# A transformer block on one core: the transposes of the softmax weights of three query heads put side by side, and their value products in the unit behind

## The chip, the cores and the metric

The kernel runs on one core of one Trainium2 chip. The metric is the device time of one execution in microseconds (us). The engines are named as the profile names them: PE (matrix products, with PEld for loading its weights), DVE (vector), ACT (scalar), POOL, and SP, which issues most DMAs. Each engine works through its own queue in order, and waits in that queue where an instruction needs the result or the freed buffer of another.

## The reference

One layer of an encoder block over 256 tokens of width 2048, in float32. Cut to what the change touches:

```python
h = rmsnorm(x); q, k, v, u = split(h @ w_in)        # 12 query heads, 4 key heads, 128 wide
scores = q @ k.T * HEAD_DIM**-0.5 - slope * |t - s|  # only |t - s| <= 128
m = max(max(scores), sink); p = exp(scores - m)
p = p / (sum(p) + exp(sink - m))
a = rmsnorm(p @ v)                                   # three query heads share a key head
f = rmsnorm(fourier_mix(u))
x = x + concat(a, f) @ w_out
x = x + conv_ffn(rmsnorm(x)); return rmsnorm(x)
```

Nothing in the mathematics is changed.

## The kernel before, in words

Every product is made of float32 halves: a weight tile of 128 x 2048 arrives by DMA, ACT rounds it to a high half and DVE subtracts to get the low half (`split`, lines 185 and 186), and PE multiplies high by high, high by low and low by high. The front of the program, up to about 215 us, is a list of numbered *units*. A unit is one such weight tile and the PE work on it. Units 4 to 7 make the values, units 8 to 23 project one key or query head each, in the order k0 q0 q1 q2 k1 q3 q4 q5 k2 q6 q7 q8 k3 q9 q10 q11 (so q3 is unit 13, q4 unit 14, q5 unit 15, k2 unit 16), and units 24 to 39 are the output projection. Behind them comes the feed-forward part, which the change does not touch.

The order is written by hand. Around the products of unit i three lists are run: `before` (PE work placed ahead of them), `beside` (the ACT and DVE work of the steps), then the split of the weights of unit i+2, then `behind`. A query head h whose projection is unit s passes through these steps:

- `qk_out` and `qk_parts` beside unit s+1: the sum `add` and the two halves of `qT`, on ACT and DVE.
- `scores` before unit s+2: six products into a bank `ps_s`; `scores_out` (DVE) beside it, and `exps` (ACT) behind it, leave the exponentials in a tile `sc`.
- `weigh` beside unit s+3: DVE divides `sc` by its sum.
- `turn` before unit s+4: four PE transposes of `sc` into a bank `ps_t` (line 712); `turn_out` beside it: ACT copies the bank to the high half `pt0`, DVE subtracts for the low half `pt1` (lines 724 and 725).
- `values` before unit s+5: six products into a bank `ps_o` (line 734); `values_out` beside it: a square on ACT that POOL adds up (lines 491 and 496), and the two halves of `cat` on ACT and DVE (lines 234 and 235), which the output projection reads.

PSUM has eight banks, in two pools of four: `mm` and `dn`. The projections take `mm`; the scores, the transposes and small sums such as `ps_totf` (the sum of squares of the Fourier part, before unit 15) take `dn`. A tile asked of a pool that has no free buffer takes the one that is freed first, and its first instruction waits for the last reader of the old tile.

Of the kernel before, what the change touches and what calls it, by code (L numbers as in the profile page):

```python
# [9 lines left out]
F32R = mybir.dt.float32r  # L10
# [3 lines left out]
P = 128  # L14
# [6 lines left out]
GQA = 3  # L21
# [30 lines left out]
N_OUT = N_QK + len(QK_ORDER)  # L52
# [44 lines left out]
def block_kernel(  # L97
# [24 lines left out]
    mm = ctx.enter_context(tc.tile_pool(name="mm", bufs=4, space=bass.MemoryType.PSUM))  # L122
    dn = ctx.enter_context(tc.tile_pool(name="dn", bufs=4, space=bass.MemoryType.PSUM))

    def f32(ap):
        return ap.bitcast(F32)
# [182 lines left out]
    ph = pa.enter_context(tc.tile_pool(name="pa", bufs=1))  # L309
# [103 lines left out]
    before, beside, behind = {}, {}, {}  # L413

    def at(when, i, f, *a):
        when.setdefault(i, []).append((f, a))
# [215 lines left out]
    def qk_out(kind, h, ps):  # L632
        tmp = ph.tile([P, S], F32, tag="tmp", name=f"tmp_{kind}{h}", bufs=2)
        nc.scalar.activation(tmp, ps[:, S : 2 * S], AF.Copy)
        add = ph.tile([P, S], F32, tag="add", name=f"add_{kind}{h}", bufs=2)
        nc.vector.tensor_tensor(add, ps[:, 0:S], tmp, ALU.add)
        if kind == "k":
            nc.vector.tensor_tensor(add, add, r1b, ALU.mult)
        st["add", kind, h] = add
# [77 lines left out]

    def turn_out(h):
        ps = st.pop(("t", h))
        pt = [  # L720
            ph.tile([P, 512], F32R, tag=f"pt{q}", name=f"pt{q}{h}", bufs=2)
            for q in range(2)
        ]
        nc.scalar.activation(pt[0], ps, AF.Copy)
        nc.vector.tensor_tensor(pt[1], ps, f32(pt[0]), ALU.subtract)
        st["p", h] = pt
# [20 lines left out]
    slot_of = {kh: N_QK + n for n, kh in enumerate(QK_ORDER)}  # L747
    for i in range(N_QK, N_OUT + 8):
        heads = {i - s: h for (kind, h), s in slot_of.items() if kind == "q"}
        new = [kh for kh, s in slot_of.items() if i - s == 1]  # L750
        if i - 9 in range(NG):
            at(before, i, fourier_channels, i - 9)
        if 5 in heads:
            at(before, i, values, heads[5], mm if i < N_OUT else dn)
        if 4 in heads:
            at(before, i, turn, heads[4])
        if i == 15:
            at(before, i, total, sq_f, "f")
        if 2 in heads:
            at(before, i, scores, heads[2])  # L760

        for kind, h in new:
            if kind == "q":
                at(beside, i, lambda k=kind, h=h: qk_out(k, h, st.pop(("ps", k, h))))
        if 4 in heads:
            at(beside, i, turn_out, heads[4])
        if 3 in heads:
            at(beside, i, weigh, heads[3])
        for kind, h in new:
            if kind == "k":  # L770
                at(beside, i, lambda k=kind, h=h: qk_out(k, h, st.pop(("ps", k, h))))
            at(beside, i, qk_parts, kind, h)
        if 2 in heads:
            at(beside, i, scores_out, heads[2])
            at(behind, i, exps, heads[2])
        if 5 in heads:
            at(beside, i, values_out, heads[5])

    fourier_channels_steps()
    for n, (kind, h) in enumerate(QK_ORDER):  # L780
# [57 lines left out]
    for n, (c, kq) in enumerate(OUT_ORDER):  # L838
        i = N_OUT + n
# [391 lines left out]
    i = up_index[n]  # L1231
# [156 lines left out]
```

## Time and profile before

| | |
|---|---|
| median of 3 runs | 906.06 us (905.99 to 906.23) |
| the profiled execution | 906.14 us, of which the span of the trace is 904.4 us |
| PE busy | 895.6 us, 99% |
| DVE, ACT, POOL busy | 745.1 us (82%), 547.2 us (61%), 51.7 us (6%) |
| HBM read | 211.93 MB, 237 GB/s over the span |

The stretch that the change touches, units 13 to 28, lies between about 80 and 185 us. In the rows of the timeline the columns are the start, the duration, engine, line, operation, the tiles (out<-in, with head numbers left out), the shape and a count; a bracket at the end names idle time ahead of the instruction and what ended it. Durations of PE overlap, since its products are pipelined: what one costs is read from the distance between starts.

### The profile page before, as it was taken

What the parts mean: (1) busy time and instruction counts of PE and PEld (TensorE: products, weight loads), DVE (VectorE), ACT (ScalarE), POOL (GpSimd) and SP (SyncE); (2) the same over time, 40 slices, a digit from 0 to 9 for tenths busy, and PEclk for the clock granted to TensorE, in tenths of its full rate; (3) what the DMA queues carried; (4) which work ended last, traced back from release to release, by engine and by line L of the source; (5) the groups of instructions that cost most, each with busy time, mean ns of one, the idle gap of its engine ahead of it and who ended that gap; (6) DMA issues with size and microseconds to landing.
All of it is one profiled execution on the core that took longest, in us unless ns stands there. A gap on an engine that the chain in (4) does not pass through costs nothing.

```text
span 904.4 us, 12754 instructions
## 1 busy us (share of the span) xinstructions
PE 895.6 (99%) x5073; PEld 811.1 (90%) x5073; DVE 745.1 (82%) x892; ACT 547.2 (61%) x663; POOL 51.7 (6%) x65
## 2 busy tenths in 40 slices
PE   9999999999999999999999999999999999999996
PEld 8899999888899999999999999999999999999885
DVE  7579888666668877889887998878988789998996
ACT  7767677555454656556565565566655566656544
POOL 0001111000000000000000000000000000000004
PEclk9999999999999999999999999999999999999999
DMA  9864544456568678677898779887787988779652
GB/s 365 332 234 145 187 152 175 146 180 226 192 231 283 231 242 251 188 257 230 275 266 271 245 258 287 258 276 237 275 250 245 312 263 262 242 240 286 217 196 94
DMA packets 32908, 214.86 MB, mean 238 GB/s; under 512 B 3632, under 2 KB 4016, under 8 KB 8528
## 3 DMA queue, kind: packets, MB, share of 16 engines
q1 hardware_dynamic: 28448, 183.89, 54.5%
q0 software_dynamic: 4112, 29.49, 17.1%
q8 instruction: 40, 0.66, 0.3%
q10 hardware_dynamic: 288, 0.66, 0.2%
q14 instruction: 20, 0.16, 0.0%
HBM read 211.93 MB, written 2.10 MB: 237 GB/s over the span
## 4 chain that ended last, share of the span: by engine, by line
PE 95%; DVE 2%; POOL 1%; issue 1%; ACT 0%; POOLq 0%; ACTq 0%; DVEq 0%
PE ps_val L394 17%; PE ps_gate L394 17%; PE ps_gate L396 8%; PE ps_val L396 8%; PE ps_q L394 5%; PE ps_P L1105 3%; PE ps_P L1107 3%; PE ps_P L1106 3%; PE ps_N L1105 2%; PE ps_N L1107 2%; PE ps_N L1106 2%; PE ps_u L286 2%; PE ps_q L396 2%; PE ps_a L377 2%; PE ps_a L379 2%; PE ps_a L378 2%
## 5 line engine op out<-in xcount | busy, mean ns | idle before, releaser
L186 DVE TENSOR_TENSOR parts<-raw,parts 128x2048 fp32r<-128x2048 f32 (+1 forms) x129 | 293.2, 2273 | 49.4 <-ACT parts L185 48.9
L185 ACT ACTIVATE parts<-raw 128x2048 fp32r<-128x2048 f32 (+1 forms) x129 | 245.4, 1902 | 46.7 <-PE ps_a L379 12.4
L394 PE MATMUL ps_val<-hU,parts 128*128 128x512 f32 x688 | 227.7, 382 | 0.0
L394 PE MATMUL ps_gate<-hU,parts 128*128 128x512 f32 x688 | 227.3, 382 | 0.0
L396 PE MATMUL ps_val<-hU,parts 128*128 128x256 f32 x688 | 187.5, 273 | 0.0
L396 PE MATMUL ps_gate<-hU,parts 128*128 128x256 f32 x688 | 186.9, 273 | 0.0
L394 PEld LDWEIGHTS ps_val<-hU,parts 128*128 128x128 f32 x688 | 130.0, 189 | 18.1
L394 PEld LDWEIGHTS ps_gate<-hU,parts 128*128 128x128 f32 x688 | 130.0, 189 | 18.1
L396 PEld LDWEIGHTS ps_val<-hU,parts 128*128 128x128 f32 x688 | 132.0, 192 | 0.8
L396 PEld LDWEIGHTS ps_gate<-hU,parts 128*128 128x128 f32 x688 | 131.8, 192 | 0.9
L883 ACT ACTIVATE ft_g<-ps_gate 128x256 f32<-128x256 f32 x43 | 16.5, 384 | 112.7 <-PE ps_gate L396 110.0
L394 PE MATMUL ps_q<-hT,parts 128*128 128x512 f32 x192 | 62.6, 384 | 0.0
L883 ACT ACTIVATE ft_v<-ps_val 128x256 f32<-128x256 f32 x43 | 16.5, 384 | 73.4 <-PE ps_val L396 73.4
L1105 PE MATMUL ps_P<-parts_P,op_P 128*128 128x512 f32 x144 | 54.7, 380 | 0.0
L1106 PE MATMUL ps_P<-parts_P,op_P 128*128 128x512 f32 x144 | 54.6, 379 | 0.0
L1107 PE MATMUL ps_P<-parts_P,op_P 128*128 128x512 f32 x144 | 54.6, 379 | 0.0
L396 PE MATMUL ps_q<-hT,parts 128*128 128x256 f32 x192 | 50.4, 273 | 0.0
L991 DVE TENSOR_TENSOR parts_N<-sumw,parts_N 128x2048 fp32r<-128x2048 f32 x18 | 41.2, 2289 | 9.9 <-ACT parts_N L990 9.9
L1105 PE MATMUL ps_N<-parts_N,op_N 128*128 128x512 f32 x108 | 41.0, 380 | 0.0
L1106 PE MATMUL ps_N<-parts_N,op_N 128*128 128x512 f32 x108 | 40.9, 379 | 0.0
L1107 PE MATMUL ps_N<-parts_N,op_N 128*128 128x512 f32 x108 | 40.9, 379 | 0.0
L394 PEld LDWEIGHTS ps_q<-hT,parts 128*128 128x128 f32 x192 | 36.1, 189 | 4.7
(346 smaller groups left out, 1557.7 us busy)
## 6 DMA issues: line engine op xcount, KB each, us to landing
raw<-in_w_up SPq DMA_DIRECT2D x86, 1024.0 KB, 6.2
raw<-in_w_in SPq DMA_DIRECT2D x20, 1024.0 KB, 5.0
sumw<-in_w_down POOLq DMA_DIRECT2D x18, 1024.0 KB, 8.5
raw<-in_w_out SPq DMA_DIRECT2D x16, 1024.0 KB, 4.8
raw<-in_w_down_late SPq DMA_DIRECT2D x4, 1024.0 KB, 5.8
u_raw<-in_u_in SPq DMA_DIRECT2D x4, 768.0 KB, 9.3
raw<-in_w_down_last SPq DMA_DIRECT2D x4, 768.0 KB, 4.2
u_raw<-in_u_in SPq DMA_DIRECT2D x6, 384.0 KB, 6.3
```

The source lines that it names most:

```text
L185: nc.scalar.activation(hi, raw, AF.Copy)
L186: nc.vector.tensor_tensor(lo, raw, f32(hi), ALU.subtract)
L286: nc.tensor.matmul(ps_u[b], block(hk(k), part, b, True), in_turn(w), start=k == 0 and n == 0, stop=k == NK - 1 and n == 2,)
L377: nc.tensor.matmul(ps, ah, wh, start=first and q == q0, stop=False)
L378: nc.tensor.matmul(ps, al, wh, start=False, stop=False)
L394: nc.tensor.matmul(ps, hi[:, s], in_turn(h), start=k == 0, stop=False)
L396: nc.tensor.matmul(ps[:, 0:S], lo[:, s], in_turn(h)[:, 0:P], start=False, stop=k == NK - 1)
L883: nc.scalar.activation(tmp, ps[:, S : 2 * S], AF.Copy)
L991: nc.vector.tensor_tensor(lo, src, f32(hi), ALU.subtract)
L1105: nc.tensor.matmul(ps, o[:, 0, p, :], wh, start=first and p == 0, stop=False)
L1106: nc.tensor.matmul(ps, o[:, 1, p, :], wh, start=False, stop=False)
L1107: nc.tensor.matmul(ps, o[:, 0, p, :], wl, start=False, stop=end)
```

## The change

The transposes of a head are no longer made four units behind its projection, and its values five behind. The three heads that share a key head are taken together: all three `turn` where the last of them had its own (before units 15, 19, 23 and 27), and all three `values` in the unit behind (16, 20, 24 and 28). `turn_out` and `values_out` move with them. No instruction is added or removed. Two choices of buffers go with it. The high half `pt0` has three buffers in place of two, and the low half `pt1` now shares the four buffers of `sc`. Of the banks of the values, the middle head's comes from `dn`, as do all from unit 24 on; the other two come from `mm`.

```diff
@@ turn_out
         pt = [
-            ph.tile([P, 512], F32R, tag=f"pt{q}", name=f"pt{q}{h}", bufs=2)
-            for q in range(2)
+            ph.tile([P, 512], F32R, tag=tag, name=f"pt{q}{h}", bufs=bufs)
+            for q, (tag, bufs) in enumerate([("pt0", 3), ("sc", 4)])
         ]
@@ the loop over the units
+        turned, valued = (
+            range(h - GQA + 1, h + 1) if (h := heads.get(late, 0)) % GQA == GQA - 1 else ()
+            for late in (4, 5)
+        )
...
-        if 5 in heads:
-            at(before, i, values, heads[5], mm if i < N_OUT else dn)
-        if 4 in heads:
-            at(before, i, turn, heads[4])
+        for h in valued:
+            at(before, i, values, h, dn if i >= N_OUT or h % GQA == 1 else mm)
+        for h in turned:
+            at(before, i, turn, h)
...
-        if 4 in heads:
-            at(beside, i, turn_out, heads[4])
+        for h in turned:
+            at(beside, i, turn_out, h)
...
-        if 5 in heads:
-            at(beside, i, values_out, heads[5])
+        for h in valued:
+            at(beside, i, values_out, h)
```

On PE, at the head of unit 15, this stood before (`o1` is the bank of the values of head 1, `t2` that of the transposes of head 2, `s3` that of the scores of head 3):

```order
L734 MATMUL ps_o1_1007<-pt01_987,v_hi_328 128x256
L734 MATMUL ps_o1_1007<-pt11_988,v_hi_328 128x256
L734 MATMUL ps_o1_1007<-pt01_987,v_lo_329 128x256
L712 MATMUL ps_t2_1014<-ident_110,sc2_911 128x128 x4
L503 MATMUL ps_totf_1019<-ones_106,sq_f_331 128x1 x2
L662 MATMUL ps_s3_1022<-kT1_908,qT3_995 128x256 x6
```

And this stands there now, at the same place of the program, with the semaphores that an instruction waits for:

```order
L712 MATMUL ps_t0_978<-ident_110,sc0_738 128x128 [waits Pool_49]
L712 MATMUL ps_t0_978<-ident_110,sc0_738 128x128 x3
L712 MATMUL ps_t1_983<-ident_110,sc1_821 128x128 [waits DVE_49,PE_49]
L712 MATMUL ps_t1_983<-ident_110,sc1_821 128x128 [waits DVE_49]
L712 MATMUL ps_t1_983<-ident_110,sc1_821 128x128 x2
L712 MATMUL ps_t2_988<-ident_110,sc2_902 128x128 [waits DVE_49] x2
L712 MATMUL ps_t2_988<-ident_110,sc2_902 128x128 x2
L503 MATMUL ps_totf_993<-ones_106,sq_f_331 128x1 [waits Pool_49]
L503 MATMUL ps_totf_993<-ones_106,sq_f_331 128x1
L662 MATMUL ps_s3_996<-kT1_899,qT3_970 128x256 [waits DVE_49]
L662 MATMUL ps_s3_996<-kT1_899,qT3_970 128x256 x5
```

Three banks `t0`, `t1`, `t2`, the bank `totf` and the bank `s3` are now asked of the pool `dn` in one go, which has four; `s3` gets the one that `t0` leaves. Its first product waits for DVE. Before, that same product waited for ACT alone.

On DVE, in units 14 and 15, this stood before (`add_q3` and `add_q4` are the sums of the projections of heads 3 and 4, `pt11` and `pt12` the low halves of heads 1 and 2, `parts16` the weights of unit 16):

```order
L636 TENSOR_TENSOR add_q3_985<-ps_q3_862,tmp_q3_983 128x256
L725 TENSOR_TENSOR pt11_988<-ps_t1_945,pt01_987 128x512
L701 TENSOR_TENSOR sm2_927<-sm2_927,ex2_928 128x2
L702 RECIPROCAL ex2_928<-sm2_927 128x2
L705 TENSOR_SCALAR sc2_911<-sc2_911,ex2_928 128x256 x2
L235 TENSOR_SCALAR qT3_995<-add_q3_985,qT3_995 128x256
L235 TENSOR_SCALAR cat0_999<-ps_o0_938,vec_87,cat0_999 128x256
L186 TENSOR_TENSOR parts16_1002<-raw16_754,parts16_1002 128x2048
L636 TENSOR_TENSOR add_q4_1064<-ps_q4_950,tmp_q4_1062 128x256
L725 TENSOR_TENSOR pt12_1067<-ps_t2_1014,pt02_1066 128x512
```

Now the subtract of head 1 and the `cat` of head 0 are gone from unit 14, and three subtracts stand together (line 726 is line 725 of before):

```order
L636 TENSOR_TENSOR add_q3_964<-ps_q3_857,tmp_q3_962 128x256
L701 TENSOR_TENSOR sm2_918<-sm2_918,ex2_919 128x2
L702 RECIPROCAL ex2_919<-sm2_918 128x2
L705 TENSOR_SCALAR sc2_902<-sc2_902,ex2_919 128x256 x2
L235 TENSOR_SCALAR qT3_970<-add_q3_964,qT3_970 128x256
L186 TENSOR_TENSOR parts16_973<-raw16_754,parts16_973 128x2048
L636 TENSOR_TENSOR add_q4_1038<-ps_q4_929,tmp_q4_1036 128x256
L726 TENSOR_TENSOR pt10_1041<-ps_t0_978,pt00_1040 128x512
L726 TENSOR_TENSOR pt11_1045<-ps_t1_983,pt01_1044 128x512
L726 TENSOR_TENSOR pt12_1049<-ps_t2_988,pt02_1048 128x512
```

The subtract of head 0, the last reader of the bank that `s3` is given, stands behind the split of unit 16's weights and the sum of head 4.

## The prediction

> **What bounds the kernel now.** I read the busy times first.
>
> ```profile
> span 904.4 us, 12754 instructions
> PE 895.6 (99%) x5073; PEld 811.1 (90%) x5073; DVE 745.1 (82%) x892; ACT 547.2 (61%) x663; POOL 51.7 (6%) x65
> ```
>
> PE is busy for all but 8.8 us of the span. Next I asked who made PE wait, in the list of waits for PE alone. It has a single row (engine and line, what it waited for, us in total, times, longest):
>
> ```profile
> PE ps_warm L229 <- POOL ones L221: 1.0, 1, 1.0
> ```
>
> So PE waits once, for 1.0 us, at the very start. Then I looked at the stretch in which the change works, in the table of stages (busy us and instructions of PE, PEld, DVE, ACT and POOL, then the granted clock, the DMA share and GB/s):
>
> ```profile
> 94.00:102.00 8.00, 8.00 (x59) 7.58 (x58) 7.09 (x13) 5.80 (x13) 1.46 (x2) 1.00 0.41 145
> ```
>
> PE has no gap there, at full clock, with DVE at 7.09 of 8 us close behind. From this follows how the change is to be weighed. It adds and removes no instruction. It can win only if the same PE instructions take less time in the new order, and it loses every microsecond for which PE waits, since no later gap in PE could take it up.
>
> **PE's own instructions: zero.** The timeline of PE around two of the transposes that move (units 14 and 15):
>
> ```profile
> 86.97 0.39 PE L734 MATMUL ps_o<-pt,v_hi 128*128 128x256 f32 x2
> ...
> 87.64 0.60 PE L712 MATMUL ps_t<-ident,sc 128*128 128x128 f32 x4
> 88.00 0.46 PE L394 MATMUL ps_q<-hT,parts 128*128 128x512 f32 x1
> 88.30 0.27 PE L396 MATMUL ps_q<-hT,parts 128*128 128x256 f32 x1
> ...
> 93.32 0.39 PE L734 MATMUL ps_o<-pt,v_hi 128*128 128x256 f32 x2
> ...
> 93.99 0.60 PE L712 MATMUL ps_t<-ident,sc 128*128 128x128 f32 x4
> 94.43 0.50 PE L503 MATMUL ps_totf<-ones,sq_f 128*128 128x1 f32 x4
> 94.79 0.91 PE L662 MATMUL ps_s<-kT,qT 128*128 128x256 f32 x6
> 95.54 0.38 PE L394 MATMUL ps_q<-hT,parts 128*128 128x512 f32 x1
> ```
>
> The values of one head take 87.64 - 86.97 = 0.67 us. Four transposes and the product behind them take 88.30 - 87.64 = 0.66. The same timeline has a place with eight transposes in a row, in the output projection:
>
> ```profile
> 228.38 1.04 PE L819 MATMUL ps_x<-ident,xs 128*128 128x128 f32 x8
> 229.17 0.46 PE L377 MATMUL ps_a<-parts,cat 128*128 128x512 f32 x1
> 229.47 0.38 PE L378 MATMUL ps_a<-parts,cat 128*128 128x512 f32 x1
> 229.69 0.38 PE L379 MATMUL ps_a<-parts,cat 128*128 128x512 f32 x1
> ```
>
> A product of 512 columns takes 229.69 - 229.47 = 0.22. Eight transposes with one such product take 1.09, so eight transposes take 0.87, and four take 0.66 - 0.22 = 0.44. Eight cost twice four, 0.11 each: a block has no price of its own for its edges, and twelve in a row will cost 1.31, what three blocks of four cost. I take zero for the regrouping. Its other bound is a gain. At the rate of 512 columns in 0.22, four transposes would take 0.22, so 0.22 to 0.23 per block is more than their columns explain. If all of that were edge, eight blocks fewer would save 8 x 0.23 = 1.8 us. The eight in a row speak against it.
>
> **The new wait.** Ahead of unit 15, PE now makes `t0`, `t1`, `t2`, `totf` and `s3` without other work between, all from a pool of four banks, and `s3` gets the bank of `t0`. That is free when DVE has subtracted the low half of head 0. So I need two times: when PE comes to `s3`, and when DVE has done that.
>
> PE: `s3` starts at 94.79 now. Out of the work ahead of it go the values of head 0 (0.67) and of head 1 (0.67), which move to unit 16. The transposes of heads 0 and 1 only move closer. PE would start `s3` at 94.79 - 1.34 = 93.45.
>
> DVE, in the same two units:
>
> ```profile
> 91.35 0.68 DVE L725 TENSOR_TENSOR pt<-ps_t,pt 128x512 fp32r<-128x512 f32 x1
> 91.95 0.15 DVE L701 TENSOR_TENSOR sm<-sm,ex 128x2 f32<-128x2 f32 x1
> ...
> 93.28 0.47 DVE L235 SCALAR_TENSOR_TENSOR cat<-ps_o,vec,cat 128x256 fp32r<-128x256 f32 x1
> 94.47 2.29 DVE L186 TENSOR_TENSOR parts<-raw,parts 128x2048 fp32r<-128x2048 f32 x1 [0.72 <-ACT parts L185]
> 96.68 0.42 DVE L636 TENSOR_TENSOR add_q<-ps_q,tmp_q 128x256 f32<-128x256 f32 x1
> 97.01 0.68 DVE L725 TENSOR_TENSOR pt<-ps_t,pt 128x512 fp32r<-128x512 f32 x1
> 97.68 0.48 DVE L235 SCALAR_TENSOR_TENSOR qT<-add_q,qT 128x256 fp32r<-128x256 f32 x1
> ```
>
> Here is the point of the whole case. DVE runs about 3 us behind PE: the bank that PE filled at 93.99 is subtracted at 97.01. Before, nobody minded, since no bank was wanted that soon. Now the subtract of head 0 takes the place of the one at 97.01, behind the split of unit 16's weights and the sum `add_q`. Two subtracts are gone ahead of it (heads 0 and 1), each 91.95 - 91.35 = 0.60, so 1.20. The `cat` at 93.28 is gone as well, but DVE then waits 0.72 for ACT's part of the split, so this counts only if ACT is earlier too:
>
> ```profile
> 91.46 0.52 ACT L234 ACTIVATE qT<-add_q 128x256 fp32r<-128x256 f32 x1 [0.75 <-DVE add_q L636]
> 91.89 0.37 ACT L491 ACTIVATE sq_a<-ps_o 128x256 f32<-128x256 f32 x1
> 92.16 0.47 ACT L234 ACTIVATE cat<-ps_o,vec 128x256 fp32r<-128x256 f32 x1
> 92.51 1.92 ACT L185 ACTIVATE parts<-raw 128x2048 fp32r<-128x2048 f32 x1
> 94.31 0.39 ACT L634 ACTIVATE tmp_q<-ps_q 128x256 f32<-128x256 f32 x1
> 94.63 0.60 ACT L724 ACTIVATE pt<-ps_t 128x512 fp32r<-128x512 f32 x1
> ```
>
> ACT's `qT` waits for DVE's `add_q`, which is 0.60 earlier (only head 0's subtract is ahead of that). Then the square and the `cat` of head 0 are gone: 92.51 - 91.89 = 0.62. ACT begins the split 1.22 earlier, and DVE's part follows it: 1.2 by either way. ACT's copy of `t0`, right behind `tmp_q`, is done before. So DVE's subtract begins at 97.01 - 1.20 = 95.81 and ends 0.68 later, at 96.49. PE waits from 93.45 to 96.49: **3.0 us**. Behind `s3` stand the 32 products of head 5's projection, whose weights are ready, and all the rest of the kernel. All of it starts 3.0 us late.
>
> Bounds of this term: if nothing moved forward on DVE, the subtract would end at 97.01 + 0.68 = 97.69, and the wait would be 4.2. If everything removed from DVE counted (1.20 and the 0.39 that `cat` took before its successor could have started), it would end at 96.10, and the wait would be 2.65. I take 3.0, since both queues give 1.2.
>
> **The other places: zero, and why.** Units 19 and 23 also turn three heads, but have no `totf`: three banks of transposes and one of scores fit in four. In unit 16, ACT, DVE and POOL get three `values_out` instead of one. `sq` has one buffer, so a square waits for POOL's addition of the one before; that adds two steps of 0.62 and at most two waits of 0.73 to ACT, 2.7 us ahead of its next split. The cover is the lead of the splits: unit 16's weights are ready at 94.47 + 2.29 = 96.76, and unit 15's projection takes PE until 95.54 + 5.24 = 100.8 (5.24 is 93.32 - 88.00 less the 0.08 that the first product ran late), so 4 us. In unit 28, the values of heads 9 to 11 take three banks of `dn`, and of the two that the output projection then asks for, the second is that of head 9, free when its `cat` is made:
>
> ```profile
> 174.78 0.73 POOL L496 TENSOR_TENSOR sq_a<-sq_a,sq 128x256 f32<-128x256 f32 x1 [5.61 <-ACT sq L491]
> 179.68 0.38 ACT L491 ACTIVATE sq<-ps_o 128x256 f32<-128x256 f32 x1 [2.81 <-PE ps_o L734]
> 180.46 0.48 DVE L235 SCALAR_TENSOR_TENSOR cat<-ps_o,vec,cat 128x256 fp32r<-128x256 f32 x1 [1.27 <-ACT cat L234]
> ```
>
> From the square to the end of `cat` is 180.94 - 179.68 = 1.3 us, and both engines had been idle before. PE asks for that bank only after twelve values (1.3 us) and twelve products of 0.22 (2.6). That is covered, as are the third head's `cat` and its two additions on POOL (0.73 each), which are needed a unit later. If the cover failed by a microsecond, it would stay within the upper bound above.
>
> Sum, against the profiled execution: 906.14 + 3.0 + 0 = 909.2. That execution is 0.08 above the median of the runs, so the median should be **909.1 us**.
>
> **Rivals.** *The clock falls as well.* Behind the last product, PE's clock goes to half:
>
> ```profile
> 896.37 0.28 PE L1255 MATMUL ps_e<-lo,act 128*128 128x256 f32 x1
> 900.00:902.00 2.00, 0.00 (x0) 0.00 (x0) 0.00 (x0) 0.00 (x0) 0.00 (x0) 0.63 0.99 378
> ```
>
> A mean of 0.63 over 2 us means full speed for 0.52 us and half speed for the rest: it fell at 900.5, 3.9 us after the last product ended at 896.65. A wait of 3.0 is shorter, so I expect no fall. If the wait reached 3.9 and the clock stayed at half for as long again, that costs 3.9 + 1.9: 912.0. The Trainium skill (TensorE: Matmul & The Clock Gate, Part 1, What's actually happening) puts the fall at an idle window of about 3.4 us, one that runs freely and need not begin with the wait; by that rule a wait of 3.0 is just too short, and the trace's 3.9 agrees with it.
>
> *No wait.* If PE did not hold at `s3`, or let the projection behind it go ahead, the 5.24 us of that projection would hide all of the wait: 906.1. Against it stands the order, in which `s3` waits for DVE, and a trace in which PE's products run in the order of the program. The same page of the Trainium skill (Step-by-step: what each phase is for) says "The MATMULs themselves stay in program order"; no run here has shown PE waiting in mid-program, so it stays a rival.
>
> *The edges count.* With the saving of 1.8 from above on top of the wait: 909.2 - 1.8 = 907.4.
>
> *Faster.* The edges count, and DVE is earlier than I work out. Its place is the same subtract; what decides is when it ends. At 93.45 or sooner there is no wait, and 906.14 - 1.8 = 904.3; at 95.3 the two cancel; later the kernel is slower. For it: DVE idles 0.72 us in unit 14, so its lag is not all load. Against it: it would have to end 3.0 us before my 96.49, and only 1.6 us of work leaves it.
>
> **How the numbers follow.** The wait alone 80%; the clock too 7%; no wait 5%; wait less edges 4%; faster 4%. The range goes from wait less edges, 907.4, to the upper bound of the wait, 906.14 + 4.2 = 910.4; it leaves out the clock, no wait and faster, 16%. A measurement of this kernel can tell about 0.2%, 1.8 us, from no change. Slower by more: the wait and the clock, 0.87. Within: no wait and wait less edges, 0.09. Faster by more: 0.04.
>
> **What would show it.** In the waits of PE one new row: `ps_s` line 662, once, about 3.0 us, ended by DVE's `pt` (line 726); nothing at units 19, 23, 27 and 28. The three blocks of transposes ahead of it start 0.44 apart. The granted clock stays 1.00 through it. I am wrong if PE shows no such wait, if a second one of like size stands in units 16 to 30, or if the twelve transposes in a row take clearly less than 1.31 us.

## The result, and the profile after

The changed kernel takes 911.0 us (median of 6 runs, 909.06 to 912.5), the kernel before 906.03 us (905.84 to 906.4): a ratio of 1.0055, with a 95% interval of 1.0042 to 1.0068. It is slower, and by more than the range that was forecast. What is striking is the spread: 3.4 us for the changed kernel, 0.6 us before. The six runs come with different mean clocks of PE: 0.998 for the run at 909.06, 0.996 for those from 910.8 to 911.0, 0.995 for those at 912.1 and 912.5.

The profile was taken of the run at 909.06. Its busy times, and the whole list of PE's waits:

```profile
span 907.3 us, 12759 instructions
PE 895.6 (99%) x5073; PEld 811.1 (89%) x5073; DVE 744.2 (82%) x892; ACT 548.1 (60%) x663; POOL 53.4 (6%) x65
```
```profile
PE ps_s L662 <- DVE pt L726: 2.9, 1, 2.9
PE ps_warm L229 <- POOL ones L221: 1.0, 1, 1.0
```

PE is as busy as before, to a tenth of a microsecond, and the span is 2.9 us longer, which is one new wait. Its place, in the timelines of PE and of DVE:

```profile
91.59 1.47 PE L712 MATMUL ps_t<-ident,sc 128*128 128x128 f32 x12
92.90 0.51 PE L503 MATMUL ps_totf<-ones,sq_f 128*128 128x1 f32 x4
96.35 0.93 PE L662 MATMUL ps_s<-kT,qT 128*128 128x256 f32 x6 [2.94 <-DVE pt L726]
```
```profile
93.07 2.29 DVE L186 TENSOR_TENSOR parts<-raw,parts 128x2048 fp32r<-128x2048 f32 x1 [1.14 <-ACT parts L185]
95.28 0.42 DVE L636 TENSOR_TENSOR add_q<-ps_q,tmp_q 128x256 f32<-128x256 f32 x1
95.61 1.88 DVE L726 TENSOR_TENSOR pt<-ps_t,pt 128x512 fp32r<-128x512 f32 x3
```

Twelve transposes take 92.90 - 91.59 = 1.31 us. `s3` then starts only at 96.35, when the first of the three subtracts, begun at 95.61, is over. So this profile shows 2.9 us of the 5. The rest is in the runs that took longer than the profiled one.

### The profile page after: what moved, and what is told of

The parts are those of the page before. It is cut to its first block, busy times and chain, and to the rows that moved or that the text cites. A ratio compares the mean times of both kernels' runs of the same rounds, so it can differ in the third digit from the quotient of the medians.

```text
span 907.3 us, 12759 instructions
## 1 busy us (share of the span) xinstructions
PE 895.6 (99%) x5073; PEld 811.1 (89%) x5073; DVE 744.2 (82%) x892; ACT 548.1 (60%) x663; POOL 53.4 (6%) x65
## 4 chain that ended last, share of the span: by engine, by line
PE 90%; DVE 4%; ACT 2%; issue 2%; POOL 1%; POOLq 0%; ACTq 0%; DVEq 0%
PE ps_val L394 17%; PE ps_gate L394 17%; PE ps_gate L396 8%; PE ps_val L396 8%; PE ps_P L1111 3%; PE ps_P L1113 3%; PE ps_P L1112 3%; PE ps_q L394 3%; PE ps_N L1111 2%; PE ps_N L1113 2%; PE ps_N L1112 2%; PE ps_u L286 2%; PE ps_a L377 2%; PE ps_a L379 2%; PE ps_a L378 2%
```

## The experiments

Three theories were set against each other. **A**: PE's clock is set anew on a beat of 3.41 us, and is at half for the beat behind one in which PE had too much idle time; so the cost of the wait depends on how the beat cuts it. **B**: a second wait, different from run to run. **C**: the clock falls when the wait is longer than some fixed length.

**The changed kernel again** (`e1`, no edit).

> The changed kernel, unchanged. Its runs lay between 909.06 and 912.5 us, with a mean granted clock of 0.998 at 909.06, 0.996 at 910.8 to 911.0 and 0.995 at 912.1 to 912.5; its profile, taken at 909.06, has the one wait of 2.9 us and a full clock. Theory A (the wait, and the clock behind it): every run waits 2.9 us, which gives 909.1; in most runs the clock then goes to half for one beat of about 3.4 us (+1.7, 910.8) or two (+3.4, 912.5). A beat of 3.41 us is read from the two traces: the time from the clock's rise to its fall is 894.29 us before and 897.71 after, 262 and 263 times 3.413. So: clusters near 909.1, 910.8 and 912.5, and a profile with the same single wait; if this profile falls on a slower run, a stretch at half clock right behind the wait. Theory B (a second wait that differs from run to run): the profile of a slower run has a further wait of 1.5 to 3.5 us in units 16 to 39, and no half clock before the end.

Measured: 910.81, 910.88, 911.07, 911.28 and 912.77 us; ratio 1.0056 (1.0043 to 1.007). This time the profile is of a longer run (911.07). Its timeline of PE:

```profile
96.67 0.94 PE L662 MATMUL ps_s<-kT,qT 128*128 128x256 f32 x6 [2.94 <-DVE pt L726]
97.44 0.38 PE L394 MATMUL ps_q<-hT,parts 128*128 128x512 f32 x1
97.66 0.27 PE L396 MATMUL ps_q<-hT,parts 128*128 128x256 f32 x1
...
98.20 0.64 PE L394 MATMUL ps_q<-hT,parts 128*128 128x512 f32 x1
98.63 0.42 PE L396 MATMUL ps_q<-hT,parts 128*128 128x256 f32 x1
98.84 0.63 PE L394 MATMUL ps_q<-hT,parts 128*128 128x512 f32 x1
...
101.40 0.38 PE L394 MATMUL ps_q<-hT,parts 128*128 128x512 f32 x1
101.62 0.27 PE L396 MATMUL ps_q<-hT,parts 128*128 128x256 f32 x1
```

The wait is the same 2.94. Behind it, a product of 512 columns takes 0.22 from start to start at first (97.44 to 97.66), then 0.43 (98.20 to 98.63), and 0.22 again from 101.40 on. The trace's record of the clock has it at half from 97.98 to 101.39, that is 3.41 us, which costs 1.7. The fall at 97.98 is 27 times 3.413 behind the clock's first rise, at 5.82. The table of stages, cut along that beat (behind the length of the stage comes PE's busy time, behind POOL's count the granted clock), first for this run, then for the profile of 909.06, where the beat is laid from the clock's own first rise at 5.94 us:

```profile
91.16:94.57 3.41, 2.57 (x22) 2.43 (x20) 2.24 (x5) 3.41 (x6) 0.00 (x0) 1.00 0.71 281
94.57:97.98 3.41, 1.31 (x9) 1.27 (x10) 3.41 (x6) 2.45 (x4) 0.00 (x0) 1.00 0.33 86
97.98:101.39 3.41, 3.41 (x12) 2.94 (x11) 3.34 (x9) 1.77 (x6) 1.91 (x1) 0.50 0.53 221
101.39:104.80 3.41, 3.41 (x25) 3.18 (x24) 0.21 (x1) 0.19 (x1) 0.80 (x1) 1.00 0.54 197
```
```profile
91.27:94.68 3.41, 2.13 (x20) 2.02 (x18) 2.27 (x4) 3.41 (x5) 0.00 (x0) 1.00 0.65 267
94.68:98.09 3.41, 1.74 (x12) 1.67 (x13) 3.41 (x7) 2.33 (x3) 0.00 (x0) 1.00 0.48 135
98.09:101.50 3.41, 3.41 (x23) 3.15 (x22) 3.12 (x8) 1.47 (x5) 2.34 (x1) 1.00 0.41 173
```

In the run at 911.07 one beat holds 2.10 us of the wait, PE is busy for 1.31 of its 3.41 us, and the next beat is at half clock. In the other, the same wait is cut into 1.27 and 1.67, no beat has under 1.74 busy, and the clock stays. So for the runs near 911 B is out: there is no second wait. Of the runs above 912 there is no trace.

**Without the wait** (`e2`).

```diff
-        if i == 15:
+        if i == 17:
             at(before, i, total, sq_f, "f")
...
-        at(beside, 15, total_scale, "f", FW)
+        at(beside, 17, total_scale, "f", FW)
```

> The changed kernel with the sum of squares of the Fourier part (ps_totf and its scale) moved from unit 15 to unit 17, so that the pool dn is asked for four banks ahead of unit 15 and not five. Theory A: the wait goes, nothing else is left: 906.0 +- 0.4 in every run, clock 0.998, no spread. Theory B: the 2.9 go, the rest of the spread stays: runs from 906.1 to 909.5. A third reading, that blocks of twelve transposes or three heads' values in one unit cost or save PE time of their own: off 906.0 by a steady amount, such as 904.2 if the edges of the blocks counted.

Measured: 906.21 us (906.01 to 906.5, 11 runs), ratio 1.0 (0.9991 to 1.0009). PE's waits:

```profile
PE ps_warm L229 <- POOL ones L221: 1.0, 1, 1.0
PE ps_u L286 <- ACT parts L274: 0.2, 1, 0.2
```

With four banks asked for and not five, the wait, the spread and the loss are all gone. The regrouping itself, twelve transposes in a row and three heads' values in one unit, costs and saves nothing that these runs can tell.

**A shorter wait** (`e3`).

```diff
-        if 2 in heads:
+        if 2 in heads and i != 15:
             at(before, i, scores, heads[2])
...
+            if (kind, h) == ("q", 5):
+                still_weights(hi, lo, ps, range(3))
+                scores(3)
+                still_weights(hi, lo, ps, range(3, NK))
+                return
```

> The changed kernel, but the scores of head 3 are put behind the first three of the sixteen steps of unit 15's projection. PE has 3 x 0.33 = 1.0 us of work to do in the wait, so 1.95 are left: 908.1 without any fall of the clock. Theory A: whether the clock falls depends on how the wait lies against the beat. In the changed kernel's profile the beat cut the wait into 1.27 and 1.67 us, and the clock stayed; so one beat must hold more than 1.67 us of idle time. A wait of 1.95 does that in about half of its positions: runs at 908.1 and at 909.8, median between. Theory C (the clock falls when a wait is longer than some fixed length between 1.95 and 2.9, wherever it lies): all runs at 908.1. Theory B: 908.1 to 911.5 with a clock of 0.998.

Measured: 908.33, 908.38, 908.84, 909.74, 909.83, 909.84 us: two clusters of three, 0.9 to 1.5 us apart; ratio 1.0031 (1.002 to 1.0043). The profile is of a run at 908.38; its wait is 1.86 us, cut into 1.50 and 0.36, and the clock stays at full. There are two clusters, as A said; the lower one lies 0.2 to 0.7 us above the 908.1 that was expected.

**A longer wait** (`e4`): two additions on DVE ahead of the subtracts.

```diff
+    def idle_adds():
+        for n in range(2):
+            junk = wp.tile([P, 512], F32, tag="junk", name=f"idle{n}")
+            nc.vector.tensor_tensor(junk, xs[0][:, 0, :], xs[0][:, 1, :], ALU.add)
...
+        if i == 15:
+            at(beside, i, idle_adds)
         for h in turned:
             at(beside, i, turn_out, h)
```

> The changed kernel with two further DVE additions of 128x512 (into a tile that nothing reads) ahead of the three subtracts of unit 15: the wait grows by about 1.1, to 4.0 us, which gives 910.2 without a fall of the clock. Theory A: some beat always holds over 1.7 us of such a wait, so the clock falls in every run: 911.9 or 913.6, none at 910.2, and the profile shows half clock right behind the wait. Theory C: the same. Theory B: 910.2 to 913.6, some runs at 910.2, clock 0.998 in the slower ones once the wait itself is taken off.

Measured: 912.47 to 913.62 us in all five runs (median 913.18), ratio 1.0075 (1.0062 to 1.0087). The wait came to 4.28 us, a little more than expected, so 910.4 would be a run without a fall; there is none. The stages along the beat, in the profile of a run at 912.82:

```profile
92.10:95.51 3.41, 1.68 (x17) 1.59 (x15) 2.28 (x2) 3.05 (x5) 0.00 (x0) 1.00 0.53 223
95.51:98.92 3.41, 0.87 (x4) 0.87 (x5) 3.38 (x7) 2.23 (x2) 0.00 (x0) 0.50 0.64 195
98.92:102.34 3.42, 3.42 (x13) 3.05 (x13) 3.13 (x10) 1.33 (x5) 1.22 (x1) 0.50 0.27 113
102.34:105.75 3.41, 3.41 (x22) 3.12 (x22) 0.90 (x1) 0.14 (x1) 1.48 (x1) 1.00 0.36 106
```

Here the first beat has 1.68 us of PE busy, 0.06 less than the beat above that kept its clock, and it is followed by half clock; the second has 0.87, and half clock lasts one more beat. That would put the limit between 1.68 and 1.74, one half of a beat, but the ends of later traces (behind `e9`) contradict this. What the first beat is busy with matters too:

```profile
91.96 1.47 PE L712 MATMUL ps_t<-ident,sc 128*128 128x128 f32 x12
93.27 0.50 PE L503 MATMUL ps_totf<-ones,sq_f 128*128 128x1 f32 x4
```

The transposes end at 91.96 + 1.47 = 93.43, which is 1.33 us into the beat. The last 0.35 of its busy time are products of a single column.

**A wait that no beat can turn into a fall** (`e5`): the edit of `e3` with 5 in place of 3.

> The changed kernel with the scores of head 3 behind the first five of the sixteen steps of unit 15's projection: 5 x 0.33 = 1.6 us of the 2.9 are filled, about 1.25 us of wait are left. So far the clock stayed in beats of 3.41 us with 1.50 and 1.67 us of idle time and fell after beats with 1.74 and 2.10. Theory A (over about 1.7 us of idle time in one beat): a wait of 1.25 can never do that, so every run gives 906.15 + 1.25 = 907.4, in one cluster no wider than the 0.5 us of the kernel before, and the profile's clock stays full. If instead any interruption over about a microsecond can drop the clock when it falls badly, there are two clusters, at 907.4 and 909.1.

Measured: 907.64 us (907.53 to 907.98, 11 runs, one cluster), ratio 1.0016 (1.0007 to 1.0025). The wait in the profile:

```profile
PE ps_s L662 <- DVE pt L726: 1.2, 1, 1.2
```

**The wait filled** (`e6`): the same with 9.

> The changed kernel with the scores of head 3 behind the first nine steps of unit 15's projection: 9 x 0.33 = 3.0 us, as long as the whole wait, which is then covered to within 0.1 us. Theory A: 906.15 to 906.3, one cluster, no row for ps_s in the waits of PE. The bank is still shared and DVE is as late as before; if it were the sharing itself or the order on DVE that costs, the time would stay near 909.

Measured: 906.38 us (906.08 to 907.09, 11 runs), ratio 1.0003 (0.9994 to 1.0012), and no row for `ps_s` in PE's waits. The bank is still shared and DVE as late as ever; given 3 us of other work on PE, neither costs anything that these runs can tell. They are not the one cluster that was expected: three of them lie 0.5 to 0.8 us above the middle of the others (906.3); why is open.

**Three single runs** (`e7`: the changed kernel; `e8`: the edit of `e3` with 2; `e9`: `e3` again), to let the rule name the outcome from the trace's beat.

> The changed kernel once more, for its trace alone. The rule drawn from the runs so far: the clock is set anew every 3.413 us, on a beat that can be laid through the trace from the clock's first rise; it is at half for the beat that follows one with over 1.7 us of idle PE time. The rule has to name the outcome from the trace's own rise and its 2.94 us of wait: a beat with under 1.67 on either side of the cut, full clock and about 909.1 us; over 1.74 on one side, half clock from the end of that beat, and 910.8 or more. Where the larger part lies ahead of the cut, half clock begins while PE still waits or has just begun again, which may make it last two beats (912.5). If instead the length of the wait alone decides, the outcome doesn't follow the cut.

> The changed kernel with the scores of head 3 behind the first two steps of unit 15's projection: a wait of 2.94 - 0.66 = about 2.25 us, a single look. By the rule of 1.7 us in one beat: no fall and 908.4 where the beat cuts it into two parts that are both under 1.7; else half clock for the beat behind, 910.1. The position is read from the trace's own first rise.

> The kernel with three steps ahead of the scores of head 3 (a wait of 1.9 us) once more, a single look. Three of its six runs were near 908.4 and three near 909.8. By the rule: 908.4 and full clock where the beat cuts the wait so that no part is over 1.7 us, else 909.8 and half clock for one beat; the trace's first rise says which it has to be.

Measured: 909.39, 908.83 and 910.01 us. The waits, in the timelines of PE of `e7`, `e8` and `e9`:

```profile
96.68 0.94 PE L662 MATMUL ps_s<-kT,qT 128*128 128x256 f32 x6 [2.95 <-DVE pt L726]
```
```profile
96.73 0.94 PE L662 MATMUL ps_s<-kT,qT 128*128 128x256 f32 x6 [2.19 <-DVE pt L726]
```
```profile
96.61 1.18 PE L662 MATMUL ps_s<-kT,qT 128*128 128x256 f32 x6 [2.00 <-DVE pt L726]
```

And the stages along each trace's beat:

```profile
91.82:95.23 3.41, 1.91 (x18) 1.82 (x16) 2.27 (x3) 3.28 (x5) 0.00 (x0) 1.00 0.60 252
95.23:98.65 3.42, 1.97 (x13) 1.87 (x14) 3.42 (x9) 2.23 (x2) 0.00 (x0) 1.00 0.54 165
98.65:102.06 3.41, 3.41 (x23) 3.14 (x22) 2.90 (x6) 1.47 (x5) 2.56 (x1) 1.00 0.34 142
```
```profile
92.24:95.65 3.41, 2.31 (x20) 1.99 (x17) 2.27 (x2) 2.91 (x5) 0.00 (x0) 1.00 0.48 204
95.65:99.06 3.41, 2.33 (x16) 2.20 (x17) 3.38 (x11) 2.23 (x2) 0.00 (x0) 1.00 0.68 216
```
```profile
93.75:97.16 3.41, 1.41 (x10) 1.09 (x9) 3.41 (x5) 2.46 (x5) 0.00 (x0) 1.00 0.24 50
97.16:100.57 3.41, 3.41 (x14) 2.96 (x12) 3.34 (x10) 2.38 (x6) 1.20 (x1) 0.50 0.65 271
```

The longest of the three waits, 2.95, is cut in the middle and costs no clock. The shortest, 2.00, lies whole in one beat and does. Theory C falls with that. `e8` came out 0.6 us above its wait alone (906.0 for the kernel before on the same chip, and 2.19). Its clock rose latest of all traces at the start, at 6.90 us against 6.22 in the trace of before; 0.68 us longer at half clock is worth 0.34 at most, so the rest stays open.

The ends of the traces hold more such beats, behind PE's last product, and they correct the limit. First the end of `e5`, then that of `e1`:

```profile
896.53:899.94 3.41, 1.52 (x14) 1.32 (x12) 1.64 (x6) 1.74 (x6) 3.18 (x4) 1.00 0.42 162
899.94:903.36 3.42, 0.00 (x0) 0.00 (x0) 1.15 (x2) 1.33 (x2) 0.06 (x1) 1.00 0.58 222
```
```profile
900.11:903.52 3.41, 1.44 (x13) 1.25 (x12) 1.56 (x6) 1.74 (x6) 3.12 (x4) 1.00 0.39 151
903.52:906.94 3.42, 0.00 (x0) 0.00 (x0) 1.15 (x2) 1.33 (x2) 0.00 (x0) 0.50 0.60 227
```

A beat with 1.52 us of busy PE (and one with 1.50 in `e8`) kept the clock, one with 1.44 lost it. So the 1.68 of `e4` fits no single limit of busy time. If the products of one column are not counted, `e4`'s beat has 1.33, and all the beats at full clock in the eleven traces fall in order: half clock behind 1.44 or less, full clock behind 1.50 or more. The transposes do count: without them the beat from 91.27 in the profile of 909.06 would have only 91.59 - 91.27 = 0.32 us of PE work besides the one-column products, and it kept the clock. All this was read from the finished traces, and no run tested it.

## Why the prediction was wrong

**PE's own instructions: zero.** Right. Twelve transposes took 1.31 us, as worked out from the block of eight, and `e2` holds the whole regrouping to 906.21 against 906.15. No edges were saved.

**The new wait.** Right in place, cause and size: it was put at 93.45 to 96.49 and 3.0 us, ended by DVE's subtract of head 0, and the profile has 93.41 to 96.35 and 2.94.

**The other places: zero.** Right. PE's list has no other new row, at units 16, 19, 23, 27 or 28.

**The clock.** Here it failed. The step was "A wait of 3.0 is shorter, so I expect no fall", with 7% for the opposite. I took the 3.9 us from PE's last product to the fall at 900.5 for the idle time that a fall needs. The traces show that the fall waits for the end of a beat: the clock's first rise at 6.2 us and its fall at 900.5 are 262 beats of 3.413 us apart. The beat from 893.7 to 897.1 still had PE busy for most of it, and the next, all idle, ended at 900.5. One such reading could not tell an idle time needed from a beat waited for. The Trainium skill (TensorE: Matmul & The Clock Gate, Part 1, What's actually happening) speaks of a window of 3413 ns that runs freely; the beat of 3.413 us agrees with that. It puts the fall behind an idle window, and I read that as a whole one. The measurements differ: beats with 1.31, 1.41 and 1.44 us of PE busy out of 3.41 were enough, those with 1.50 and 1.52 were not, so somewhat over half a beat of idle time suffices. With half a beat as the limit, a wait of 2.94 escapes only if the beat cuts it into two parts that are both under 1.7, which is 2 x 1.71 - 2.94 = 0.48 of 3.41 positions, one in seven. With 1.9 as the limit and the 0.35 of one-column products ahead of the wait counted as idle, it is 2 x 1.9 - 3.29 = 0.51, much the same. Two of the twelve runs of the changed kernel escaped (909.06 and 909.39). The first of them is the run of the first profile: that it agrees with the forecast of 909.1 is luck.

So the term that was missing from the sum is 1.7 us, half of one beat: 906.1 + 2.9 + 1.7 = 910.7, and seven of the twelve runs lie 0.1 to 0.6 above that (910.79 to 911.28). I had the price of a fall about right (1.9) but tied it to a wait of 3.9. Three runs lie at 912.1 to 912.8, as if half clock had lasted two beats. None of the traces of the changed kernel caught one; the trace of `e4` shows that a second beat with little busy time (0.87) prolongs it. The start of the program suggests that a beat with far more does so too, since at half clock more busy time was needed to raise the clock than was needed to keep it. In `e8` six products of 512 columns start 0.41 us apart from 4.70 on, so the clock is still low there, although PE had been busy for 2.50 us in the beat from 0.07 to 3.49. In `e3` a beat with 3.14 us raised it. So a slow beat that still holds 0.9 us of the wait may be followed by another; its 2.5 us of work at half clock cost 1.25 more, and 906.1 + 2.9 + 1.25 + 1.7 = 912.0 is near the three runs. No trace of such a run exists, and it stays open.

## What to carry to other kernels

Before work is packed together on the busiest engine, count the buffers that the pack asks for in one go, and look up how far behind the engine that frees them is running: a lag of 3 us that never shows as a wait becomes one as soon as one buffer is missing. Here one small sum moved by two units, or nine steps of ready work put ahead of the blocked product, takes all of it back. And a gap on PE is to be priced with its clock. Here a wait of 1.2 us cost itself alone in all eleven runs, one of 1.9 to 2.0 cost about 1.4 more in four of seven, and one of 2.9 cost 1.7 or more on top in ten of twelve. Which of these it is depends on how the beat cuts the wait, so a single profile can show the cheap case.

## What the runs showed of the hardware

PE's clock is decided on a fixed beat of 3.413 us that is laid by its first rise in the trace (rise to last fall: 262 or 263 beats, as the traces of before and after have it). In eight traces with a wait, half clock followed the beats around the wait with 0.87, 1.31, 1.41 and 1.68 us of busy PE, and full clock those with 1.74 or more. At the ends of the traces, a beat with 1.44 lost the clock and beats with 1.50 and 1.52 kept it, so busy time alone isn't quite the measure. Half clock begins at the end of the beat, in `e1` 1.3 us after PE is back at work, and the products that are slow stand where nothing waits: the list of waits doesn't show this loss, only the granted clock and the distance between starts do.
